# Interleaving VectorE's seven-product work across pairs, with more seven-product pairs: a two-layer decoder trunk on one core

## The chip, the cores and the metric

The kernel runs on one core of a Trainium2 chip. The metric is the device time in microseconds of one execution, given as the median of three runs. TensorE (PE) multiplies matrices, VectorE (DVE), ScalarE (ACT) and GpSimd (POOL) work elementwise, and SyncE (SP), like POOL, issues transfers. Every engine takes its instructions in the order of its own list and waits on semaphores for the others.

## The reference

The model has two layers on 256 positions of width 2048. Each layer is a token mixer (HGRN2 in the first, gated linear attention in the second) beside a cross-attention into 256 memory positions, an output projection, and a SwiGLU feed-forward of width 5632:

```python
h = x
for layer in range(DEPTH):
    hn = _rmsnorm(h, norm_mix[layer])
    ...
    h = h + jnp.concatenate([y, xa], axis=-1) @ w_out[layer]
    hn = _rmsnorm(h, norm_ffn[layer])
    gate, up = jnp.split(hn @ w_gate_up[layer], 2, axis=-1)
    h = h + (jax.nn.silu(gate) * up) @ w_down[layer]
return _rmsnorm(h, norm_final)
```

In the second mixer one input projection gives keys, queries, values, gates, a low-rank decay and the attention's queries. All is float32.

## The kernel before, in words

**Three matmuls for one product.** To keep float32 accuracy each operand is held as two fp32r tiles, a rounded high half and the rest as a low half. A product is three matmuls into one PSUM bank: high by high, high by low, low by high. The activations are split once. The weights stream in from HBM and every weight tile is split as it comes: ScalarE writes the high half (a cast), VectorE writes the low half (source minus high half). `split` (L276) does both. The result is a tile `parts`; the code names the splits of weight tile number i `parts{i}a` to `parts{i}d`.

**Seven products for eight.** A pair is 256 rows of weights by two column ranges of 512 (gate and up in the feed-forward; keys and queries, or two heads' columns, in a mixer), that is four 128x512 blocks in one tile `raw`. With the two halves of the 256 positions, a pair is a 2x2 by 2x2 product of blocks: eight products in the plain way. In the Strassen-Winograd way there are seven, each of 128 rows of weights, at the cost of sums of weight blocks. `seven` (L451) makes them: it splits the first block (part a) and the third and fourth (part b), subtracts the first block (`raw` 128x512), subtracts that from the third and fourth (`raw` 128x1024), and splits the results (part c with the sign turned, part d). For `fed` pairs the sum of two blocks is made on the way in, by a POOL transfer that adds to what an SP transfer has put there (L443, L444). For the first pair of a block, and for the last where it is of this kind, that sum sits in a tile of its own (`apart`, tile `T`), loaded long ahead.

A pair's kind is a letter. S is seven products, 21 matmuls. O is eight products from two splits. H is eight products too, but with sums that suit the banks of S; it takes splits a and b, one subtraction of 512 columns, and split c of that, 24 matmuls in all. In the mixers "-" is the plain form, 24 matmuls.

**Feed-forward.** `ffn` (L1208) goes over eleven blocks of 512 gate and 512 up columns. `up_block` calls `project_halves` (L624), which goes over the eight pairs of the block with the kinds in `KINDS` (L1197), one string each for the blocks 0, 1, 2 and 3 and one for all later blocks. The seven sums in PSUM are put together by `sums` (seven VectorE additions from PSUM), then gate times up is formed (`gate`), turned, and split as the left operand of the down projection. Two pieces of the down projection (`down`) follow each block from the second on; their weights are split into four or eight plain parts. In blocks 1 and 2 such a piece is 24 matmuls by two, later twice as long. The first block has no down projection behind it, and the second sums up the first block's products after its own first pair: `WHEN` says after which pair each of these works is due.

**What sets the order.** From the fourth pair of a layer's first block on, `Engine.kept` keeps each engine's instructions in the order in which the code is written. Elsewhere a scheduler may move them.

**Buffers.** `raw` has three buffers. Splits of two blocks share six buffers (`parts`); splits of one block, which are part a of an S pair and part c of an H pair, share two (tag `part`, L288). A cast into such a buffer waits until TensorE has used what was there before.

**Second mixer.** `gla_pair` (L1067) runs twice. Each run projects keys and queries for two heads with `project_two` (L549), 384 columns each, with the plan `------S-`: seven plain pairs and one S, in which the sum of two blocks is made by VectorE (`fed=False`).

Of the kernel before, what the change touches and what calls it, by code (L numbers as in the profile page):

```python
# [17 lines left out]
P = 128  # L18
# [22 lines left out]
def trunk_kernel(ctx: ExitStack, tc: tile.TileContext, x, mem, norm_mix, norm_ffn, norm_mem,  # L41
# [234 lines left out]
    def split(src, name, by=2, turned=False):  # L276

        if isinstance(src, list):
            both = wts.tile([P, 2, 2, 512], F32R, tag="parts", name=f"parts{name}", bufs=6)
            for k in (1, 0):  # L280
                hi = both[:, 0, k:k + 1, :]
                ac.activation(out=hi, in_=src[k], func=AF.Copy, scale=-1.0)
                ve.scalar_tensor_tensor(out=both[:, 1, k:k + 1, :], in0=src[k], scalar=-1.0, in1=hi.bitcast(F32),
                                        op0=ALU.mult, op1=ALU.subtract)
            return [(both[:, 0, k, :], both[:, 1, k, :]) for k in range(2)]
# [165 lines left out]
    def seven(i, raw, fed, between=None):  # L451

        n = raw.shape[2]
        tt = ve.tensor_tensor
        b00, = split(raw[:, 0:1, :], f"{i}a")
        b11, b10 = split(raw[:, 2:4, :], f"{i}b")
        if between:
            between()

        if not fed:  # L460
            tt(out=raw[:, 1, :], in0=raw[:, 1, :], in1=raw[:, 2, :], op=ALU.add)
        apart = fed if fed and fed is not True else None
        tt(out=raw[:, 0, :], in0=apart[:, 0, :] if apart else raw[:, 1, :], in1=raw[:, 0, :], op=ALU.subtract)
        tt(out=raw[:, 2:4, :], in0=raw[:, 2:4, :], in1=raw[:, 0:1, :].broadcast_to([P, 2, n]), op=ALU.subtract)
        t6, t7 = split([raw[:, 0:1, :], apart] if apart else raw[:, 0:2, :], f"{i}c", turned=True)
        t5, t4 = split(raw[:, 2:4, :], f"{i}d")
        return {1: ("x00", b00), 2: ("x01", b10), 3: ("z", b11), 4: ("x11", t4), 5: ("s", t5), 6: ("u", t6), 7: ("d0", t7)}
# [81 lines left out]
    def project_two(pairs, plan, w, c0, c1, n, name, give, view=lambda ps: ps, onto=None, prep=None, behind=None,  # L549
# [43 lines left out]
        for at, (p, kind) in enumerate(zip(order, plan)):  # L593
            i, raw = new_raw()
            if i == 0:
                load_pair(raw, w, p, c0, c1, n, kind, fed)
            if prep:
                prep(at)
            if i > 0:
                load_pair(raw, w, p, c0, c1, n, kind, fed)  # L600
            if kind == "S":
                todo = held(behind, seven, i, raw[:, :, 0:n], fed) if behind else seven(i, raw[:, :, 0:n], fed)
# [21 lines left out]
    def project_halves(forms, kinds, w, c0, c1, name, key, keep, apart):  # L624
# [15 lines left out]
        for p, kind in enumerate(kinds):  # L640
            Engine.kept = keep <= p
# [3 lines left out]
            fed = apart.get(p, True)  # L645
            load_pair(raw, w, p, c0, c1, 512, kind, fed)
            x = forms[p].get
            last = p == len(PAIRS) - 1
            if kind == "S":
                todo = seven(i, raw, fed, lambda: mark(key + p))  # L650
                for b in (1, 2, 6, 7, 5, 4, 3) if last else (1, 3, 2, 6, 7, 5, 4):
                    product(b, x(todo[b][0]), todo[b][1])
            else:
                b00, b01 = split(raw[:, 0:2, :], f"{i}a")
# [412 lines left out]
    def gla_pair(w, pr, dec, decay, hq, r, yq):  # L1067
# [46 lines left out]
        project_two(hq["pairs"], ("------S-", "------S-")[pr], w, kw + pr * 2 * DK, pr * 2 * DK, 2 * DK, f"gk{pr}", give,  # L1114
# [82 lines left out]
    KINDS = ("SHHSHOSO", "HHHSSOSO", "SHHSSOSO", "SSHSSOHS", "SSSSSOSS")  # L1197
# [10 lines left out]
    def ffn(l, forms, r, after, tail=None):  # L1208
# [9 lines left out]
        def up_block(b):  # L1218
# [5 lines left out]
            def sums():  # L1224
# [4 lines left out]
                for out, p, q in ((s0, 2, e0), (e1, 6, e0), (s1, 7, e1), (e1, 5, e1), (e0, 5, s1),  # L1229
                                  (s1, 4, s1), (e1, 3, e1)):  # L1230
                    ve.tensor_tensor(out=out, in0=ps[p], in1=q, op=ALU.add)
                    if p in (2, 5) and out is not e0 and b:
                        free_port.append(ve.last)
# [200 lines left out]
```

## Time and profile before

| what | before |
|---|---|
| median of three runs | 2255.65 us (2253.49 to 2257.12) |
| the profiled execution, its own time | 2254.6 us |
| its span, first to last instruction | 2252.8 us |
| granted TensorE clock | 0.999 |
| matmuls | 10668 |
| TensorE, VectorE, ScalarE, GpSimd busy | 99%, 90%, 64%, 12% of the span |
| feed-forward of the first layer | about 517 to 1181 us |
| feed-forward of the second layer | about 1560 to 2250 us |
| second mixer's two key/query stages | 1231.5 to 1275.6 and 1356.8 to 1392.3 us |

A row of the timeline has the start in microseconds, the length, the engine, the line, the operation, out<-in, the size, and in brackets how long the engine had been idle before it and who released it. Nearly all lines read L151, the helper through which every instruction is issued, so pieces are told apart by their tiles' names. `f_p` are the banks of the feed-forward's products and `hf_0` to `hf_7` the split activations of the eight pairs. Matmuls overlap, so the length of one row is longer than its share of time; the distance from start to start is what counts. Layer by layer the feed-forward has the same pattern, 204 weight tiles and 1043.3 us apart.

### The profile page before, as it was taken

Reading aid. Unit: us, or ns where it says so; the run is one execution under the profiler, and the core shown is the slowest. Engines: PE = TensorE matmul, PEld = TensorE weight load, DVE = VectorE, ACT = ScalarE, POOL = GpSimd, SP = SyncE. Lnnn points to the kernel's source line nnn. Section 1 sums busy time; section 2 is a strip of 40 time slices with the busy share of each in tenths; the row PEclk is TensorE's granted clock in tenths of the full one; section 3 lists DMA queues with packets and bytes.
Section 4 is the critical chain, followed back from the end, with each engine's and each line's share of the span. In section 5 each row is a group of like instructions: output and inputs, shape, how many; then the busy total and the mean of one; then the engine's idle time right before and its main releaser. Section 6 shows DMA issues by size and latency. Waiting matters only on the chain.

```text
span 2252.8 us, 30400 instructions
## 1 busy us (share of the span) xinstructions
PE 2238.6 (99%) x10668; PEld 1894.6 (84%) x10668; DVE 2031.5 (90%) x2551; ACT 1452.8 (64%) x2010; POOL 280.4 (12%) x275
## 2 busy tenths in 40 slices
PE   9999999999999999999999999999999999999998
PEld 7888888888888888888889999988888888888887
DVE  6879899898998999999996887889999999999997
ACT  7656656565666666666665665566566676666664
POOL 1000100000111112112210000000011221212110
PEclk9999999999999999999999999999999999999999
DMA  8656655656687778878865445566677878887874
GB/s 296 215 168 213 199 182 177 200 193 190 198 236 232 229 234 231 230 230 238 244 221 168 141 156 182 164 209 197 208 221 224 233 230 238 242 238 236 231 233 167
DMA packets 255628, 477.28 MB, mean 212 GB/s; under 512 B 18255, under 2 KB 47731, under 8 KB 255219
## 3 DMA queue, kind: packets, MB, share of 16 engines
q1 hardware_dynamic: 228547, 420.21, 55.5%
q0 software_dynamic: 25632, 50.87, 13.0%
q10 hardware_dynamic: 1296, 4.26, 0.5%
q8 instruction: 84, 1.38, 0.2%
q14 instruction: 69, 0.57, 0.1%
HBM read 472.12 MB, written 3.15 MB: 211 GB/s over the span
## 4 chain that ended last, share of the span: by engine, by line
PE 90%; DVE 6%; issue 2%; DMA 1%; ACT 1%; SPq 0%; POOL 0%; DVEq 0%; POOLq 0%; ACTq 0%
PE f_p L151 34%; PE fd L151 18%; PE wo L151 4%; PE m1p L151 2%; PE hv2p L151 2%; PE hv1p L151 2%; PE hf0p L151 2%; PE hv0p L151 2%; PE wo1p L151 2%; PE hf2p L151 2%; PE hf1p L151 2%; PE wo0p L151 2%; PE m0p L151 2%; PE gk0p L151 1%; PE gk1p L151 1%
## 5 line engine op out<-in xcount | busy, mean ns | idle before, releaser
L151 DVE TENSOR_TENSOR raw<-raw 128x1024 f32<-128x1024 f32 (+3 forms) x330 | 311.2, 943 | 16.7 <-DMA raw<-in_w_down_dram 5.6
L151 ACT CAST parts<-raw 128x1024 fp32r<-128x1024 f32 (+1 forms) x216 | 211.7, 1016 | 56.8 <-DMA raw<-in_w_down_dram 14.7
L151 DVE TENSOR_TENSOR parts<-raw,parts 128x1024 fp32r<-128x1024 f32 (+1 forms) x176 | 200.2, 1171 | 22.7 <-ACT parts L151 22.0
L444 POOL DMA_DIRECT2D raw<-in_w_gate_up_dram x92 | 80.4, 873 | 541.2 <-DMA raw<-in_w_gate_up_dram 274.7
L300 POOL TENSOR_TENSOR parts<-raw,parts 128x1024 fp32r<-128x1024 f32 x40 | 95.6, 2406 | 113.5 <-ACT parts L151 81.2
L151 ACT COPY h<-fd 128x512 f32<-128x512 f32 x80 | 45.7, 588 | 46.5 <-PE fd L151 44.0
L428 POOL DMA_DIRECT2D T<-in_w_gate_up_dram x36 | 21.1, 587 | 430.2 <-DVE hf_4g L151 82.7
L151 ACT ACTIVATE s<-s,rf_r 128x512 f32<-128x512 f32 x44 | 31.8, 723 | 42.0 <-DVE s L151 42.0
L151 DVE SCALAR_TENSOR_TENSOR s<-e,rf_r,s 128x512 f32<-128x512 f32 x44 | 45.7, 1076 | 2.9 <-ACT s L151 0.5
L151 DVE TENSOR_TENSOR e<-f_p,e 128x512 f32<-128x512 f32 x66 | 45.2, 684 | 2.6 <-DVE s L151 0.5
L429 POOL DMA_DIRECT2D T<-in_w_gate_up_dram x36 | 31.0, 861 | 120.4 <-DMA T<-in_w_gate_up_dram 111.1
L151 ACT COPY fd<-h 128x512 f32<-128x512 f32 x82 | 45.2, 582 | 0.0
L444 POOL DMA_DIRECT2D raw<-in_hgrn_w_in_dram x17 | 14.7, 867 | 209.9 <-DMA raw<-in_hgrn_w_in_dram 124.6
L151 PE MATMUL fd<-parts,s_0h 128*128 128x512 f32 x128 | 39.8, 392 | 0.0
L151 PE MATMUL fd<-parts,s_4h 128*128 128x512 f32 x128 | 39.8, 392 | 0.0
L151 PE MATMUL fd<-parts,s_8h 128*128 128x512 f32 x128 | 39.8, 392 | 0.0
L151 PE MATMUL fd<-parts,s_2h 128*128 128x512 f32 x128 | 39.8, 392 | 0.0
L151 PE MATMUL fd<-parts,s_6h 128*128 128x512 f32 x128 | 39.8, 392 | 0.0
L151 PE MATMUL fd<-parts,s_1h 128*128 128x512 f32 x128 | 39.4, 389 | 0.0
L151 PE MATMUL fd<-parts,s_3h 128*128 128x512 f32 x128 | 39.4, 389 | 0.0
L151 PE MATMUL fd<-parts,s_5h 128*128 128x512 f32 x128 | 39.4, 389 | 0.0
L151 PE MATMUL fd<-parts,s_7h 128*128 128x512 f32 x128 | 39.4, 389 | 0.0
(6020 smaller groups left out, 7434.0 us busy)
## 6 DMA issues: line engine op xcount, KB each, us to landing
raw<-in_w_gate_up_dram SPq DMA_DIRECT2D x224, 512.0 KB, 4.4
raw<-in_w_down_dram SPq DMA_DIRECT2D x80, 1024.0 KB, 5.5
raw<-in_w_gate_up_dram SPq DMA_DIRECT2D x220, 256.0 KB, 4.2
raw<-in_hgrn_w_in_dram SPq DMA_DIRECT2D x79, 512.0 KB, 4.6
raw<-in_gla_w_in_dram SPq DMA_DIRECT2D x96, 384.0 KB, 3.3
raw<-in_w_gate_up_dram POOLq DMA_DIRECT2D x92, 256.0 KB, 4.9
T<-in_w_gate_up_dram POOLq DMA_DIRECT2D x72, 256.0 KB, 5.0
raw<-in_w_out_dram SPq DMA_DIRECT2D x16, 1024.0 KB, 5.1
```

Of the source, the lines that this page charges most:

```text
L151: ins = func(*args, **kwargs)
L300: low = (nc.gpsimd if free_port else ve).tensor_tensor(out=both[:, 1, k:j, 0:m], in0=src[:, k:j, :], in1=both[:, 0, k:j, 0:m].bitcast(F32) ...
L428: nc.gpsimd.dma_start(out=both[:, 0, :], in_=rows[0])
L429: nc.gpsimd.dma_start(out=both[:, 0, :], in_=rows[1], accum_op=ALU.add)
L444: nc.gpsimd.dma_start(out=raw[:, 1, 0:n], in_=rows[1], accum_op=ALU.add)
```

## The change

It does five things.

1. In `seven`, the steps are put in another order, and the next pair is begun before this one is finished: after split c, a new argument `ahead` allocates and loads the next pair's tile and makes its split a; only then comes split d. A pair that was begun so goes on with the 512-wide subtraction before split b. The 1024-wide subtraction and split c change places with regard to what lies between them, so that no step stands right behind the one whose result it needs.
2. The same in H pairs: the next pair's split a stands between the subtraction and split c.
3. In `project_two`, an S pair that follows an S pair is begun early in the same way. This touches every stage that has two S pairs in a row.
4. `KINDS` gets two more S pairs in each of the blocks 0 and 1 and one more in each of the blocks 2 and 3 of both layers, each in the place of an H pair. The later blocks' string is the same. The two key/query stages get a second S pair in the place of a plain one.
5. `sums` takes bank 6 before bank 2 and swaps two later additions.

```diff
-    def seven(i, raw, fed, between=None):
+    def seven(i, raw, fed, between=None, b00=None, ahead=None):
...
-        b00, = split(raw[:, 0:1, :], f"{i}a")
...
+        def less():
+            tt(out=raw[:, 0, :], in0=apart[:, 0, :] if apart else raw[:, 1, :], in1=raw[:, 0, :], op=ALU.subtract)
+
+        def both_less():
+            tt(out=raw[:, 2:4, :], in0=raw[:, 2:4, :], in1=raw[:, 0:1, :].broadcast_to([P, 2, n]), op=ALU.subtract)
+
+        if not begun:
+            b00, = split(raw[:, 0:1, :], f"{i}a")
+        if not fed:
+            tt(out=raw[:, 1, :], in0=raw[:, 1, :], in1=raw[:, 2, :], op=ALU.add)
+        if fed and begun:
+            less()
         b11, b10 = split(raw[:, 2:4, :], f"{i}b")
         if between:
             between()
...
+        if not (fed and begun):
+            less()
+        if apart:
+            t6, t7 = split([raw[:, 0:1, :], apart], f"{i}c", turned=True, between=both_less)
+        else:
+            both_less()
+            t6, t7 = split(raw[:, 0:2, :], f"{i}c", turned=True)
+        if ahead:
+            ahead()
         t5, t4 = split(raw[:, 2:4, :], f"{i}d")
...
+        def ahead(p):
+            if p < len(PAIRS):
+                i, raw = come(p)
+                came.append((i, raw, split(raw[:, 0:1 if kinds[p] == "S" else 2, :], f"{i}a")))
...
                     ve.tensor_tensor(out=raw[:, 3, :], in0=raw[:, 3, :], in1=raw[:, 2, :], op=ALU.subtract)
+                    ahead(p + 1)
                     e1, = split(raw[:, 3:4, :], f"{i}c")
...
-        project_two(hq["pairs"], ("------S-", "------S-")[pr], w, kw + pr * 2 * DK, pr * 2 * DK, 2 * DK, f"gk{pr}", give,
+        project_two(hq["pairs"], "-----SS-", w, kw + pr * 2 * DK, pr * 2 * DK, 2 * DK, f"gk{pr}", give,
...
-    KINDS = ("SHHSHOSO", "HHHSSOSO", "SHHSSOSO", "SSHSSOHS", "SSSSSOSS")
+    KINDS = ("SHSSSOSO", "SHSSSOSO", "SSHSSOSO", "SSSSSOHS", "SSSSSOSS")
...
-                for out, p, q in ((s0, 2, e0), (e1, 6, e0), (s1, 7, e1), (e1, 5, e1), (e0, 5, s1),
+                for out, p, q in ((e1, 6, e0), (s0, 2, e0), (s1, 7, e1), (e0, 5, s1), (e1, 5, e1),
```

What this does to the order is shown at three places of the first layer. Weight tiles 84 to 91 are the pairs of its block 0, 92 to 99 those of block 1, 102 to 109 those of block 2.

VectorE in block 0, from the fourth pair (87) on; `hf0_7g` and `hf0_7l` are steps of the last pair's activations. Before:

```order
L151 TENSOR_TENSOR parts87a_4541<-raw87_4536,parts87a_4541 128x512
L151 TENSOR_TENSOR hf0_7g_4488<-hf0_7g_4488 128x256
L151 SCALAR_TENSOR_TENSOR hf0_7g_4488<-hf0_7g_4488 128x128
L151 TENSOR_TENSOR hf0_7g_4488<-hf0_7g_4488 128x128
L151 TENSOR_TENSOR parts87b_4544<-raw87_4536,parts87b_4544 128x1024
L151 TENSOR_TENSOR hf0_7l_4482<-hf0_7g_4488,hf0_7h_4481 128x1024
L151 TENSOR_TENSOR raw87_4536<-raw87_4536 128x512
L151 TENSOR_TENSOR hf0_7g_4488<-hf0_7g_4488 128x128
L151 TENSOR_TENSOR raw87_4536<-raw87_4536 128x1024
L151 SCALAR_TENSOR_TENSOR parts87c_4549<-raw87_4536,parts87c_4549 128x1024
L151 TENSOR_TENSOR hf0_7l_4482<-hf0_7g_4488,hf0_7h_4481 128x128
L151 TENSOR_TENSOR parts87d_4552<-raw87_4536,parts87d_4552 128x1024
```

And after:

```order
L151 TENSOR_TENSOR parts87a_4520<-raw87_4515,parts87a_4520 128x512
L151 TENSOR_TENSOR raw87_4515<-raw87_4515 128x512
L151 TENSOR_TENSOR hf0_7g_4496<-hf0_7g_4496 128x256
L151 TENSOR_TENSOR parts87b_4548<-raw87_4515,parts87b_4548 128x1024
L151 SCALAR_TENSOR_TENSOR hf0_7g_4496<-hf0_7g_4496 128x128
L151 TENSOR_TENSOR raw87_4515<-raw87_4515 128x1024
L151 TENSOR_TENSOR hf0_7g_4496<-hf0_7g_4496 128x128
L151 SCALAR_TENSOR_TENSOR parts87c_4552<-raw87_4515,parts87c_4552 128x1024
L151 TENSOR_TENSOR parts88a_4560<-raw88_4555,parts88a_4560 128x512
L151 TENSOR_TENSOR parts87d_4563<-raw87_4515,parts87d_4563 128x1024
L151 TENSOR_TENSOR hf0_7l_4490<-hf0_7g_4496,hf0_7h_4489 128x1024
L151 TENSOR_TENSOR raw88_4555<-raw88_4555 128x512
```

The first split of pair 88, now an S pair, stands ahead of the last split of pair 87, and the longest step of the activations has moved behind it.

VectorE in block 1, from split a of its fourth pair (95) on, which was and is an S pair; `s0_0l` belongs to block 0's down projection. Before:

```order
L151 TENSOR_TENSOR parts95a_4861<-raw95_4856,parts95a_4861 128x512
L151 TENSOR_TENSOR parts95b_4864<-raw95_4856,parts95b_4864 128x1024
L151 TENSOR_TENSOR s0_0l_4819<-tp_s0_0h_48180_4820,s0_0h_4818 128x512
L151 TENSOR_TENSOR raw95_4856<-raw95_4856 128x512
L151 TENSOR_TENSOR raw95_4856<-raw95_4856 128x1024
L151 SCALAR_TENSOR_TENSOR parts95c_4871<-raw95_4856,parts95c_4871 128x1024
L151 TENSOR_TENSOR parts95d_4874<-raw95_4856,parts95d_4874 128x1024
L151 TENSOR_TENSOR parts96a_4905<-raw96_4900,parts96a_4905 128x512
```

And after:

```order
L151 TENSOR_TENSOR parts95a_4854<-raw95_4849,parts95a_4854 128x512
L151 TENSOR_TENSOR parts94d_4857<-raw94_4799,parts94d_4857 128x1024
L151 TENSOR_TENSOR raw95_4849<-raw95_4849 128x512
L151 TENSOR_TENSOR parts95b_4882<-raw95_4849,parts95b_4882 128x1024
L151 TENSOR_TENSOR s0_0l_4839<-tp_s0_0h_48380_4840,s0_0h_4838 128x512
L151 TENSOR_TENSOR raw95_4849<-raw95_4849 128x1024
L151 SCALAR_TENSOR_TENSOR parts95c_4888<-raw95_4849,parts95c_4888 128x1024
L151 TENSOR_TENSOR parts96a_4896<-raw96_4891,parts96a_4896 128x512
L151 TENSOR_TENSOR parts95d_4899<-raw95_4849,parts95d_4899 128x1024
L151 TENSOR_TENSOR raw96_4891<-raw96_4891 128x512
```

The two `raw` steps are apart, and between split c and split d of a pair stands split a of the next.

ScalarE in block 2, around the pairs 105 and 106. Before:

```order
L151 CAST parts105a_5288<-raw105_5283 128x512
L151 CAST parts105b_5291<-raw105_5283 128x1024
L151 ACTIVATE parts105c_5296<-raw105_5283 128x1024
L151 CAST parts105d_5299<-raw105_5283 128x1024
L151 CAST parts106a_5328<-raw106_5323 128x512
```

And after:

```order
L151 CAST parts105a_5279<-raw105_5274 128x512
L151 CAST parts104c_5282<-raw104_5240 128x512
L151 CAST parts105b_5310<-raw105_5274 128x1024
L151 ACTIVATE parts105c_5314<-raw105_5274 128x1024
L151 CAST parts106a_5322<-raw106_5317 128x512
L151 CAST parts105d_5325<-raw105_5274 128x1024
```

The cast of parts106a, whose buffer is one of the two, has moved ahead of that of parts105d. The second layer has the same orders, with the tiles' numbers 204 higher.

More of the change, by code (lines that the diff above doesn't have):

```diff
@@ L591, in early, with come @@
                 out[:] = onto
[L593 removed]
+        came = []
+        def come(at):
             i, raw = new_raw()
             if i == 0:
[L596 removed]
+                load_pair(raw, w, order[at], c0, c1, n, plan[at], fed)
             if prep:
@@ L649, in project_halves @@
             if kind == "S":
-                todo = seven(i, raw, fed, lambda: mark(key + p))
+                todo = seven(i, raw, apart.get(p, True), lambda: mark(key + p), begun and begun[0], lambda: ahead(p + 1))
                 for b in (1, 2, 6, 7, 5, 4, 3) if last else (1, 3, 2, 6, 7, 5, 4):
@@ L653, in project_halves @@
             else:
-                b00, b01 = split(raw[:, 0:2, :], f"{i}a")
+                b00, b01 = begun or split(raw[:, 0:2, :], f"{i}a")
                 mark(key + p)
```

37 lines of the change are left out of this document (23 added, 14 removed).

## The prediction

> All times are microseconds of the one core; a pair is named by the number of its weight tile (raw 84 is the first of the first feed-forward layer), its parts by the letters of the code.
>
> **What bounds the kernel now.** First the page: which engine is busy, and for how long.
>
> ```profile
> span 2252.8 us, 30400 instructions
> ...
> PE 2238.6 (99%) x10668; PEld 1894.6 (84%) x10668; DVE 2031.5 (90%) x2551; ACT 1452.8 (64%) x2010; POOL 280.4 (12%) x275
> ```
>
> TensorE is taken all the time and VectorE nearly so. Whether TensorE waits inside its 99% is told by the chain of waits: length by number of matmuls.
>
> ```profile
> 729.83 38.81 PE f_p L151 x171
> ...
> 1367.88 24.47 PE gk1p L151 x141
> ```
>
> 38.81 / 171 = 0.227 for a 512-wide matmul, 24.47 / 141 = 0.173 for a 384-wide one, with nothing between them. There each matmul left out is time won, as long as VectorE delivers the parts in time. So the second view is VectorE's timeline, for one seven-product pair (S) where such pairs follow one another:
>
> ```profile
> 733.78 0.68 DVE L151 TENSOR_TENSOR parts126a<-raw,parts126a 128x512 fp32r<-128x512 f32 x1
> 734.38 1.22 DVE L151 TENSOR_TENSOR parts126b<-raw,parts126b 128x1024 fp32r<-128x1024 f32 x1
> 735.51 1.94 DVE L151 TENSOR_TENSOR raw<-raw 128x512 f32<-128x512 f32 x2
> 737.46 1.23 DVE L151 SCALAR_TENSOR_TENSOR parts126c<-raw,parts126c 128x1024 fp32r<-128x1024 f32 x1
> 738.65 1.23 DVE L151 TENSOR_TENSOR parts126d<-raw,parts126d 128x1024 fp32r<-128x1024 f32 x1
> 739.79 0.68 DVE L151 TENSOR_TENSOR parts127a<-raw,parts127a 128x512 fp32r<-128x512 f32 x1
> ```
>
> From start to start a 512-wide step takes 0.60 and a 1024-wide one 1.14. The pair lasts 6.01, of which 2 x 0.60 + 4 x 1.14 = 5.76 is the steps; 0.25 goes where a step needs the one just before it (the two raw steps take 1.95, not 1.74). TensorE needs 21 x 0.227 = 4.77 for the same pair: in a run of S pairs VectorE loses 1.2 a pair, and lives on the lead it gains in the down projections. The third view is the same for an eight-product pair (H):
>
> ```profile
> 568.11 1.23 DVE L151 TENSOR_TENSOR parts94a<-raw,parts94a 128x1024 fp32r<-128x1024 f32 x1 [0.26 <-ACT parts94a L151]
> 569.25 1.22 DVE L151 TENSOR_TENSOR parts94b<-raw,parts94b 128x1024 fp32r<-128x1024 f32 x1
> 570.50 0.69 DVE L151 TENSOR_TENSOR raw<-raw 128x512 f32<-128x512 f32 x1
> 571.96 0.69 DVE L151 TENSOR_TENSOR parts94c<-raw,parts94c 128x512 fp32r<-128x512 f32 x1 [0.77 <-ACT parts94c L151]
> 572.57 0.69 DVE L151 TENSOR_TENSOR parts95a<-raw,parts95a 128x512 fp32r<-128x512 f32 x1
> ```
>
> 4.46, with 2 x 1.14 + 2 x 0.60 = 3.48 of steps; the rest is waiting for ScalarE. TensorE needs 24 x 0.227 = 5.45 for it. And the place where VectorE's lead is spent, a few pairs on, on TensorE's timeline:
>
> ```profile
> 584.26 0.50 PE L151 MATMUL f_p<-parts96c,hf_4h 128*128 128x512 f32 x1 [0.35 <-DVE parts96c L151]
> ...
> 586.90 0.61 PE L151 MATMUL f_p<-parts97a,hf_5h 128*128 128x512 f32 x2
> ```
>
> TensorE waits for parts96c: in the second block VectorE is the one that comes last, and it is only just in time. (The wait falls on a part's second matmul, which takes the low half that VectorE writes.) So two engines bound this kernel: TensorE nearly everywhere, VectorE in the first two blocks of each layer, where the change puts eight of its twelve new S pairs.
>
> **What it removes.** An H pair made S drops a product, three matmuls: 12 pairs x 3 x 0.227 = 8.2. The two key/query stages drop one product each: 2 x 3 x 0.173 = 1.04. Together 9.2, all on the path if the parts are in time.
>
> **What it adds, first two blocks.** By the steps above an S pair costs VectorE 5.76 (interleaved) where the H pair cost 4.46, and an H pair that stays falls to 3.48. What that makes is counted over the stretch from parts87a, the first part of the fourth pair, to the end of pair 96.
>
> ```profile
> 528.30:586.50 58.20, 57.85 (x258) 47.19 (x258) 53.47 (x62) 34.63 (x43) 3.47 (x4) 1.00 0.59 182
> ```
>
> ```profile
> 528.31 0.69 DVE L151 TENSOR_TENSOR parts87a<-raw,parts87a 128x512 fp32r<-128x512 f32 x1 [1.32 <-ACT parts87a L151]
> ...
> 558.28 0.68 DVE L151 TENSOR_TENSOR s<-f_p,e 128x512 f32<-128x512 f32 x1
> ...
> 564.53 1.22 DVE L151 TENSOR_TENSOR parts93b<-raw,parts93b 128x1024 fp32r<-128x1024 f32 x1
> ...
> 585.32 1.22 DVE L151 TENSOR_TENSOR parts97a<-raw,parts97a 128x1024 fp32r<-128x1024 f32 x1
> ```
>
> Before, VectorE took 58.2 from 528.31 to the end of parts97a (586.54), for 30 steps of 1024, 26 of 512 and five short ones of the last forms (1.2 together, an estimate by width from the 0.60): 34.2 + 15.6 + 1.2 = 51.0. The other 7.2 were waits (the row above has VectorE busy for 53.47 of 58.20; a record reaches some 0.09 into the next one). In the new order parts97a stands ahead of parts96d, so the stretch ends with parts96d; it holds 35 of 1024, 28 of 512 and the same five: 39.9 + 16.8 + 1.2 = 57.9. So the waits that interleaving wins back are eaten by the added steps. I leave 0.9 of waits in it: 0.2 in pair 90, which follows an O pair and is not begun early; about 0.15 in H pair 93; and 0.5 in the sums and gate, which take 6.25 before (558.28 to 564.53) for nine steps of 0.60, and lose a little by their new order. That makes 58.8. From below the waits can be 0, from above the 7.2 of before; I take 0.9 since the waits in the rows above are all of the kinds that the new order parts.
>
> The start shifts too. Parts a of an S pair and part c of an H pair share two buffers (tag "part"). Before, parts87a took the buffer of parts85c:
>
> ```profile
> 527.65 0.62 ACT L151 CAST parts87a<-raw 128x512 fp32r<-128x512 f32 x1 [1.93 <-PE f_p L151]
> ...
> 624.76 0.62 ACT L151 CAST parts105a<-raw 128x512 fp32r<-128x512 f32 x1 [1.04 <-PE f_p L151]
> ```
>
> Now it takes that of parts86a, which is free three matmuls (0.68) into pair 86:
>
> ```profile
> L151 PE MATMUL f_p<-parts86a,hf_2h x8: 387/394/476, 527.8 to 530.2; 128*128 128x512 f32 x8
> ```
>
> So its cast starts at 528.5 instead of 527.65, with the copies of the last form and parts87c queued behind it on ScalarE, and VectorE starts at about 529.2. 529.2 + 58.8 = 588.0: parts96d is complete. TensorE can start its first matmul 0.23 before that and needs six (1.36) to finish the pair: 589.2 against 586.90 before, **2.3 later**. Without VectorE it would have been 4 x 0.68 = 2.7 earlier; 5.0 of waits take the place. What is late next is parts c and d, put back by the 0.60 or 1.14 of the next pair's first split.
>
> **Third block.** One more S pair: 0.68 less. VectorE has lead here, but after H pair 104 the two buffers bind: parts106a must wait for TensorE's first product from parts105a, and parts105d now stands behind it on ScalarE and VectorE.
>
> ```profile
> 629.96 0.62 PE L151 MATMUL f_p<-parts105a,hf_3h 128*128 128x512 f32 x2
> ```
>
> With 2.3 of delay and 0.68 saved pair 105 starts at 631.5 and frees the buffer at 632.2. ScalarE casts 106a (0.62, as in the row above) and 105d (about 1.1, an estimate from twice the width), to 633.9; VectorE then does 105d, raw 0.60, 106b, raw, 106c, 107a, 106d: 6 x 1.14 + 0.60 more, 641.3. TensorE would want parts106d's low half at 631.5 + 4.77 + 5 x 0.68 + 0.23 = 639.9. A wait of 1.35, so +0.67 in all; between 0 (the lead suffices) and 2.
>
> **Fourth block**: 0.68 less, no H pair ahead of two S pairs, VectorE's lead large: -0.68. **Later blocks** have the same pairs as before: each S pair is 0.25 shorter, part d comes 0.6 to 1.1 later; nothing to win, since TensorE does not wait there. Sum for a layer: 2.3 + 0.67 - 0.68 = +2.3, for both +4.6.
>
> **Key/query stages.** The first one's busy row (PE, PEld, DVE, ACT, POOL after the length), and its steps:
>
> ```profile
> 1231.00:1276.00 45.00, 45.00 (x260) 43.64 (x259) 34.45 (x60) 29.10 (x50) 1.09 (x3) 1.00 0.44 140
> ```
>
> ```profile
> 1273.73 0.55 DVE L151 TENSOR_TENSOR gsk<-gk0p,gsq 128x384 f32<-128x384 f32 x1
> 1274.19 0.95 DVE L151 TENSOR_TENSOR parts232b<-raw,parts232b 128x768 fp32r<-128x768 f32 x1
> ```
>
> The new S pair needs three 384-wide (0.46) and four 768-wide (about 0.87) steps, 4.9, for the two 768-wide ones before, 1.7: +3.1 on an engine with 10.5 idle in 45. I take them as hidden: -1.04 for both; at worst two thirds uncovered, +2; at best, with the final adds no longer mixed with the decay chain, -2.
>
> **Transfers and queues.** A feed-forward pair made S has one more issue on SP and an accumulating one on POOL:
>
> ```profile
> raw<-in_w_gate_up_dram SPq DMA_DIRECT2D x220, 256.0 KB, 4.2
> ...
> raw<-in_w_gate_up_dram POOLq DMA_DIRECT2D x92, 256.0 KB, 4.9
> ```
>
> 4.2 + 4.9 and the hand-over is some 10 from the release of the tile; between release and use lie two pairs, 3.48 + 5.76 = 9.2 at the shortest, and in the first and second block the sums or the early load besides. Nothing, at most 0.8 a place without that cover. The other S runs (first mixer, output, memory) are interleaved too; TensorE does not wait there, so nothing.
>
> **The sum.** The profiled execution took 2254.6, 1.8 beyond its span. +4.6 - 1.04 = +3.5: 2258.1. The median of the runs is 2255.65, 1.05 above the profiled one; on its scale **2259.2**. That is +0.16%; a measurement of this kernel tells about 0.2% (4.5) from nothing. Case chance 0.56, own range 2254 to 2264.
>
> **Rivals.** (1) Faster: VectorE keeps up and the 9.2 arrive, 2246.5. For it: the blocks from the fifth on carry seven S pairs each with TensorE unbroken (38.81 for 171), and 7.2 of waits lie in the stretch. Against it: the count, 57.9 of pure steps where TensorE would be done at 584.2. It needs parts96d 5 earlier. 0.18, part of it only halfway (2251).
> (2) Slower, by the two buffers: in each chain H, S, S of the first three blocks the second S is held as in the third. One wait of 1.35 is counted; two more a layer are 2 x 2.7 = 5.4: 2264.6. It decides if the cast of parts95a starts after TensorE's first product from parts94a rather than right after parts94c's cast. For it: both bracketed rows <-PE f_p. Against it: by the count VectorE reaches parts95a about 1 after that product. 0.14.
> (3) Slower: taking needy neighbours apart wins nothing, S stays 6.01 and H 4.46. Five begun S pairs (0.25) and one H (1.0) in the stretch, one S after it, 2.5 a layer: 2264.2. Against it: the raw steps' 1.95 for 1.74. 0.12.
> The Trainium skill ("VectorE: DVE Perf Modes", The DRAIN you can't avoid) speaks for this: the next VectorE operation waits for the pipe to empty whatever it needs, and a semaphore between two costs nothing more. The rows do not agree: the step behind one that it needs starts 0.2 later.
>
> **How the numbers follow.** The forecast's case lies within 2251.1 to 2260.2 for 0.36 of its 0.56; rival 1 gives 0.17 below and the rest inside; rivals 2 and 3 and the forecast's remainder lie above. Faster 0.17, same 0.38, slower 0.45. The range leaves out the lower half of rival 1 and the worst of leftover waits (3 more a layer): 2249 to 2267.
>
> **What would show it.** TensorE waiting for parts87d to 88d and 94c to 96d in both layers, some 5 a layer; parts96d complete near 588 if the span's start is alike; parts106a's cast held by TensorE; f_p unbroken in the fourth block and later. Wrong if parts96d comes before 584, if the waits stand at parts a or b (transfers), or if the key/query stages move by more than 2.

## The result, and the profile after

The changed kernel takes **2272.3 us** (median of five runs, 2270.75 to 2273.87), the kernel before 2255.65: ratio 1.0078, 95% interval 1.0064 to 1.0092. The forecast was 2259.2, its range ended at 2267. Slower was its likeliest side, but the size was wrong, and the largest part of the loss lies where the prediction had put nothing.

The page of the changed kernel (span; then busy time, share and instructions of each engine) says little by itself:

```profile
span 2272.0 us, 30459 instructions
...
PE 2241.0 (99%) x10626; PEld 1883.1 (83%) x10626; DVE 2053.3 (90%) x2587; ACT 1465.7 (65%) x2028; POOL 295.2 (13%) x289
```

42 matmuls are gone, as planned, and TensorE is at 99% as before; the span is 19.2 longer. Where that comes from is told by the windows, cut at the first matmul of the same weight tiles: 84 to 102 (the first two blocks), 102 to 112 (the third), 112 to 124 (the fourth), 124 to 208 (the seven later ones). Columns: start:end, length, busy time and instructions of PE, PEld, DVE, ACT, POOL, granted clock, DMA share, GB/s. The first layer before:

```profile
516.80:614.30 97.50, 97.15 (x439) 79.86 (x438) 87.57 (x105) 61.23 (x81) 9.56 (x8) 1.00 0.62 196
614.30:666.90 52.60, 52.60 (x238) 43.63 (x237) 47.83 (x52) 35.25 (x47) 10.35 (x9) 1.00 0.79 236
666.90:729.70 62.80, 62.80 (x283) 52.09 (x282) 56.66 (x63) 40.19 (x52) 11.63 (x12) 1.00 0.79 236
729.70:1159.90 430.20, 430.20 (x1926) 356.56 (x1925) 408.56 (x441) 290.60 (x369) 80.48 (x73) 1.00 0.80 234
```

And after:

```profile
517.80:618.20 100.40, 96.67 (x427) 77.07 (x426) 95.49 (x114) 64.30 (x86) 16.35 (x14) 1.00 0.71 211
618.20:672.50 54.30, 52.91 (x235) 42.87 (x235) 49.35 (x53) 36.22 (x47) 10.45 (x9) 1.00 0.75 224
672.50:736.40 63.90, 62.90 (x279) 51.25 (x278) 58.71 (x65) 41.05 (x53) 11.93 (x11) 1.00 0.78 231
736.40:1169.80 433.40, 432.15 (x1927) 356.12 (x1926) 406.08 (x441) 292.19 (x371) 80.87 (x73) 1.00 0.79 234
```

The first layer is longer by 2.9, 1.7, 1.1 and 3.2, the second, cut at the same tiles, by 3.0, 1.1, 1.1 and 2.8: 16.9 in all, about the 16.65 between the medians. The last row is the one to read twice. In the later blocks the strings are the same, VectorE is busy for 2.5 *less* than before, and the stretch is 3.2 longer. No work was added there; it is done in another order.

The chain of waits (start, length, what) of the changed kernel shows the place. Where it ran through 171 matmuls at a stretch before, it now crosses to VectorE once in each later block:

```profile
758.14 1.23 DVE parts128d L151
759.42 16.43 PE f_p L151 x71
...
821.33 16.43 PE f_p L151 x71
```

Parts128d is the last part of the last of five S pairs in a row; an O pair (129) follows. VectorE's timeline before, and TensorE's first use of that part:

```profile
750.70 1.23 DVE L151 TENSOR_TENSOR parts128d<-raw,parts128d 128x1024 fp32r<-128x1024 f32 x1
751.84 1.22 DVE L151 TENSOR_TENSOR parts129a<-raw,parts129a 128x1024 fp32r<-128x1024 f32 x1
```

```profile
752.14 0.62 PE L151 MATMUL f_p<-parts128d,hf_4h 128*128 128x512 f32 x2
```

The part was complete at 751.93, 0.2 ahead of its first matmul and, with 0.23 from matmul to matmul, 0.4 ahead of the second, which takes the low half. So before there was no wait, but hardly a lead either. The same places after:

```profile
757.01 1.22 DVE L151 TENSOR_TENSOR parts129a<-raw,parts129a 128x1024 fp32r<-128x1024 f32 x1
758.14 1.22 DVE L151 TENSOR_TENSOR parts128d<-raw,parts128d 128x1024 fp32r<-128x1024 f32 x1
```

```profile
758.87 0.39 PE L151 MATMUL f_p<-parts128d,hf_4h 128*128 128x512 f32 x1
759.42 0.50 PE L151 MATMUL f_p<-parts128d,hf_4h 128*128 128x512 f32 x1 [0.16 <-DVE parts128d L151]
```

The next pair's split a takes the turn of split d, which starts 1.13 after it. The matmul that needs the low half comes 0.33 late and the one behind it 0.11 more: 0.44 in a block, seven blocks, two layers, 6.2. The changed kernel pays this for a part (129a) that is first used 2.5 after it is complete.

### The profile page after: what moved, and what is told of

Read it like the earlier page. It is cut to its first block, busy times and chain, and to the rows that moved or that the text cites. A ratio compares the mean times of both kernels' runs of the same rounds, so it can differ in the third digit from the quotient of the medians.

```text
span 2272.0 us, 30459 instructions
## 1 busy us (share of the span) xinstructions
PE 2241.0 (99%) x10626; PEld 1883.1 (83%) x10626; DVE 2053.3 (90%) x2587; ACT 1465.7 (65%) x2028; POOL 295.2 (13%) x289
## 4 chain that ended last, share of the span: by engine, by line
PE 48%; DVE 16%; issue 8%; DMA 3%; ACT 2%; SPq 0%; ACTq 0%; DVEq 0%; POOLq 0%; POOL 0%
PE fd L151 17%; PE f_p L151 16%; DVE raw L151 3%; PE wo L151 2%; PE wo1p L151 2%; DMA raw<-in_w_gate_up_dram 2%; PE gg11p L151 1%; PE gg01p L151 1%; PE gg10p L151 1%; PE gk1p L151 1%; PE gx L151 1%; PE gk0p L151 1%; PE fd_0p L151 1%; DMA raw<-in_w_down_dram 1%; DVE parts L151 0%
## 5 line engine op out<-in xcount | busy, mean ns | idle before, releaser
L151 DVE TENSOR_TENSOR raw<-raw 128x512 f32<-128x512 f32 (+2 forms) x346 | 328.1, 949 | 21.1 <-DMA raw<-in_w_down_dram 7.8
L446 POOL DMA_DIRECT2D raw<-in_w_gate_up_dram x102 | 88.3, 865 | 609.7 <-DVE raw L151 303.1
L430 POOL DMA_DIRECT2D T<-in_w_gate_up_dram x38 | 24.5, 645 | 339.4 <-DVE ro_v L151 56.9
L151 DVE SCALAR_TENSOR_TENSOR s<-e,rf_r,s 128x512 f32<-128x512 f32 x44 | 54.1, 1269 | 2.5
L431 POOL DMA_DIRECT2D T<-in_w_gate_up_dram x38 | 32.8, 862 | 128.5 <-DMA T<-in_w_gate_up_dram 99.7
```

The lines of the kernel that those rows point to most:

```text
L151: ins = func(*args, **kwargs)
L430: nc.gpsimd.dma_start(out=both[:, 0, :], in_=rows[0])
L431: nc.gpsimd.dma_start(out=both[:, 0, :], in_=rows[1], accum_op=ALU.add)
L446: nc.gpsimd.dma_start(out=raw[:, 1, 0:n], in_=rows[1], accum_op=ALU.add)
```

## The experiments

The table has the lengths of the eight stretches, cut as above, from each run's own trace, one execution each; "before" in a run's text is the median of the kernel before on the same chip.

| kernel | first layer | second layer | sum |
|---|---|---|---|
| before | 97.5, 52.6, 62.8, 430.2 | 97.3, 52.8, 62.8, 430.5 | 1286.5 |
| the change | 100.4, 54.3, 63.9, 433.4 | 100.3, 53.9, 63.9, 433.3 | 1303.4 |
| the new order alone | 98.6, 55.4, 64.0, 433.2 | 99.5, 54.0, 64.0, 433.1 | 1301.8 |
| the added pairs alone | 101.2, 51.9, 62.8, 430.5 | 101.1, 52.0, 64.6, 430.3 | 1294.4 |
| S pairs begin only S pairs early | 99.7, 53.1, 63.0, 430.6 | 99.7, 52.9, 63.1, 430.1 | 1292.2 |
| the same with the old strings | 96.8, 52.9, 63.1, 430.1 | 96.7, 53.0, 63.1, 430.5 | 1286.2 |
| 1024-wide step between the halves of split c | 97.4, 52.5, 62.9, 432.0 | 97.3, 52.5, 62.9, 432.2 | 1289.7 |
| H pairs only, tile 103 made S | 96.8, 51.9, 62.8, 432.4 | 96.7, 52.2, 62.8, 432.3 | 1287.9 |
| the same, old order inside S | 96.7, 51.9, 62.8, 430.1 | 96.8, 51.9, 62.7, 430.5 | 1283.4 |
| the same, tile 88 made S too | 96.0, 52.7, 62.7, 430.6 | 96.1, 51.9, 62.7, 430.2 | 1282.9 |
| the change, H pairs only | 98.2, 51.9, 64.3, 432.3 | 98.5, 51.9, 64.3, 432.2 | 1293.6 |
| the change, split c of H pairs in a wide buffer | 99.7, 54.9, 63.9, 433.2 | 99.2, 54.1, 63.9, 433.2 | 1302.1 |
| key/query pairs alone | 97.3, 52.6, 62.7, 430.4 | 97.3, 53.9, 62.8, 430.4 | 1287.4 |
| key/query pairs, third and fourth block | 97.3, 52.2, 62.8, 430.2 | 97.3, 51.9, 63.1, 430.2 | 1285.0 |

**The new order alone.**

```diff
-    KINDS = ("SHSSSOSO", "SHSSSOSO", "SSHSSOSO", "SSSSSOHS", "SSSSSOSS")
+    KINDS = ("SHHSHOSO", "HHHSSOSO", "SHHSSOSO", "SSHSSOHS", "SSSSSOSS")
```

and the key/query plan of before.

> The changed kernel with the kinds of pairs of before (feed-forward strings and key/query plan); only the order is new. Theory A (two costs: a next pair's split a ahead of split d makes d late at the end of every run of S pairs; and added S pairs overfill VectorE): the seven later blocks of each layer lose 0.44 each as in the changed kernel, 6.2 in all, at TensorE's wait for part d of their fifth pair, and the chains H, S, S of the second to fourth block lose up to 1.9 each by the held split a: 2262 to 2270. Theory B (only the added S pairs cost; the order is neutral or better): 2252 to 2256, with no wait at part d in the later blocks.

2271.18 (before 2255.84): ratio 1.0059, interval 1.0045 to 1.0072: against theory B, and a little above theory A's range. The order by itself costs nearly all that the change costs. The wait at the fifth pair of each later block is there:

```profile
759.54 0.50 PE L151 MATMUL f_p<-parts128d,hf_4h 128*128 128x512 f32 x1 [0.17 <-DVE parts128d L151]
```

**The added pairs alone**, in the order of before (the change's strings and plan in the kernel before).

> The kernel before with the new strings and the new key/query plan, each pair in the old order. Theory A: no wait in the later blocks; an S pair costs VectorE 1.55 more than the H pair it replaces (6.01 for 4.46), three of them in the stretch to the end of pair 96 whose lead is used up: 4 to 5 later per layer there, the third block about 0, the fourth up to 0.7 later, key/query 1.0 earlier: 2262 to 2267. Theory B: the old order loses more than the new, so above the changed kernel's 2272. Theory C (the order alone is at fault): the products left out arrive, 2247 to 2251.

2261.26 (before 2255.84): 1.0024, 1.0015 to 1.0033; a little under theory A's range, far from B and C. The later blocks are untouched. The loss is in the first two blocks (+3.7 and +3.8); in the third each layer wins 0.7 to 0.8; the fourth wins nothing in the first layer and loses 1.8 in the second. The list of TensorE's waits (who, for whom: us, times, longest):

```profile
PE f_p L151 <- DVE parts95c L151: 0.8, 1, 0.8
PE f_p L151 <- DVE parts299c L151: 0.8, 1, 0.8
...
PE f_p L151 <- DVE parts94c L151: 0.8, 1, 0.8
...
PE f_p L151 <- DVE parts88c L151: 0.8, 1, 0.8
```

These are waits for part c in the blocks where VectorE had no lead. The two effects overlap: 15.3 and 5.4 apart, 16.6 together.

**S pairs begin only S pairs.**

```diff
-  ... begun and begun[0], lambda: ahead(p + 1))
+  ... begun and begun[0], (lambda: ahead(p + 1)) if kinds[p + 1:p + 2] == "S" else None)
```

> The changed kernel, but an S pair begins the next pair ahead of its own split d only where the next is an S pair too; ahead of an O or H pair split d comes first, as before. Theory A: the 0.44 of each later block goes (6.2 in all), and of the waits for the last part d of a run in the first four blocks (88d, 96d, 106d, 116d: 0.78, 0.79, 0.78, 0.76) up to 3.1 a layer: 2260 to 2266. Theory B: VectorE's count of steps is the same, so 2270 to 2273.

2262.75 (before 2255.84): 1.0029, 1.0019 to 1.0039, within theory A's range. Of the 16.65 above the kernel before 6.9 are left: 9.7 (11.2 of the 16.9 in the table) are gone by this one condition, with VectorE busy for 2053.1, as with the change (2053.3). The 6.9 are near the 5.4 of the added pairs alone. At the end of the run the two splits stand the old way round, and the later blocks take 430.6 and 430.1:

```profile
754.06 1.22 DVE L151 TENSOR_TENSOR parts128d<-raw,parts128d 128x1024 fp32r<-128x1024 f32 x1
755.21 1.22 DVE L151 TENSOR_TENSOR parts129a<-raw,parts129a 128x1024 fp32r<-128x1024 f32 x1
```

**The same condition with the strings and the plan of before.**

> The strings and the key/query plan of before, and the new order with an S pair begun early only by an S or H pair, an O or H pair never begun ahead of split d of an S pair. By the waits of the run with the new order alone: 0.44 at each of fourteen later blocks goes, and 0.52, 0.78, 0.76 and 0.76 at parts 87d, 96d, 106d and 116d of each layer, 11.8 in all: 2259 to 2262, with the waits at 105c, 105d and 106c left. If the order loses by something else (transfers asked for later, the sums' new order): 2265 to 2271.

2257.88 (before 2254.9): 1.001, 1.0001 to 1.0018; better than expected by 1. It is 3.0 above its own before where the new order alone was 15.3 above its own, so 12.4 of what the order costs by the medians, and all that it costs in the table's stretches, hang on beginning an O or H pair ahead of split d. The new order of the sums (item 5) and the early S pairs of the mixers (item 3) were not run alone; this kernel has both, and with all that is left of the order it is 3.0 slower. No wait over 0.24 is left in the first layer's `f_p`; a new one stands in the first layer's last down projection (0.7 in the second layer's):

```profile
PE fd_0p L151 <- DVE parts210c L151: 1.3, 1, 1.3
```

**The second S pair of the key/query stages alone.**

> The kernel before with the second S pair in the two key/query stages alone. Theory A (VectorE's idle time there covers it): 1.0 less, 2254.6, the stage 43.6 long for 44.1. Rival (the added 3.1 of VectorE's work delays what follows, the value stage above all): 2255.5 to 2257.

2256.95 (before 2255.84): 0.9999, 0.9991 to 1.0008: no gain that can be told. The stages show what happens. The first and the stretch behind it, before:

```profile
1231.50:1275.50 44.00, 44.00 (x254) 42.86 (x254) 33.45 (x58) 28.60 (x49) 1.09 (x3) 1.00 0.43 137
...
1275.50:1356.80 81.30, 79.71 (x482) 77.47 (x481) 72.73 (x129) 53.81 (x83) 1.73 (x4) 1.00 0.52 168
```

and in the changed kernel:

```profile
1240.60:1284.10 43.50, 43.50 (x251) 42.20 (x250) 33.87 (x59) 28.58 (x50) 1.09 (x3) 1.00 0.44 141
1284.10:1366.70 82.60, 80.93 (x481) 77.27 (x481) 74.47 (x132) 54.70 (x85) 1.74 (x4) 1.00 0.51 165
```

In the changed kernel 0.5 is won in the stage and 1.3 lost behind it; with this edit alone the two are 44.0 and 82.0. The loss behind it does not come each time: cut at the stage's own matmuls, the run with the added pairs alone, which has the same edit, takes 43.4 and 81.5 where the kernel before takes 43.8 and 81.5. Its cause is not shown.

**Split c of an H pair in a wide buffer.**

```diff
-                    e1, = split(raw[:, 3:4, :], f"{i}c")
+                    e1, = split(raw[:, 3:4, :], f"{i}c", wide=True)
```

> The changed kernel, but split c of an H pair takes one of the six wide buffers, so that the two small ones serve the parts a of S pairs alone. If the hold by the two buffers is what the third block loses by, the cast of parts106a starts right behind parts105c, and of the waits at parts b, c and d of pair 106 (0.21, 0.88 and 0.78) some 1.2 goes in each layer: 2269 to 2271. If VectorE's count and split d behind the next split a are the cause there too: 2271.5 to 2273.

2271.1 (before 2254.9): 1.0065, 1.0049 to 1.0081, not to be told from the change. The hold is gone, and something else takes its place. In the change the third block has, on ScalarE and VectorE,

```profile
633.45 0.62 ACT L151 CAST parts106a<-raw 128x512 fp32r<-128x512 f32 x1 [2.56 <-PE f_p L151]
```

```profile
637.20 0.69 DVE L151 TENSOR_TENSOR raw<-raw 128x512 f32<-128x512 f32 x1 [0.92 <-DMA raw<-in_w_gate_up_dram]
```

and here

```profile
631.17 0.62 ACT L151 CAST parts106a<-raw 128x512 fp32r<-128x512 f32 x1 [1.80 <-DMA raw<-in_w_gate_up_dram]
```

```profile
636.38 0.69 DVE L151 TENSOR_TENSOR raw<-raw 128x512 f32<-128x512 f32 x1 [2.37 <-DMA raw<-in_w_gate_up_dram]
```

The cast no longer waits for TensorE, and VectorE waits 2.37 instead of 0.92 for the tile's accumulating transfer. Tile 106 takes the memory of tile 103, which is free when split d of 103 is done, and that split, too, stands behind the next split a in this order. Counted from the first matmul of tile 84 this subtraction of tile 106 starts after 119.4 in both kernels, so the buffers were one of two equal limits there. That the place of split d makes the transfer late was not tested. The transfer can come late without the change too: in the run with the key/query pairs alone, which leaves this block as it was, VectorE waited for it in the second layer,

```profile
1679.22 1.95 DVE L151 TENSOR_TENSOR raw<-raw 128x512 f32<-128x512 f32 x2 [1.46 <-DMA raw<-in_w_gate_up_dram]
```

and that layer's third block took 53.9 for 52.8. Differences of 1 in this block are therefore not put down to an edit without such a row.

**Only H pairs begin the next pair early**, with the strings of the change.

> The new strings and plan; only H pairs begin the next pair early, S pairs do not, and split c of an H pair has a wide buffer. If beginning a pair early inside a run of S pairs is worth its 0.14 a pair, this is no better than the run with S pairs begun only ahead of S pairs (2262.75); if the delay of split d by 0.6 costs more than that, it is at or below the run with the added pairs alone: 2258 to 2261.

2265.27 (before 2254.9): 1.0042, 1.0028 to 1.0056. This is no better than 2262.75, as the first theory said, and worse than the added pairs alone. But its later blocks took 432.3 and 432.2, where nothing begins early and nothing was added: something else in the order inside S pairs costs time too. The next run shows the same with only one pair added in each layer.

**H pairs only, old strings, and one S pair more (tile 103).** The sums and the key/query plan are those of before, and split c of an H pair has a wide buffer.

> The kernel before with H pairs alone beginning the next pair early, split c of an H pair in a wide buffer, and one added S pair: the second of the third block (tile 103), where no wait followed it in the run with the added pairs alone. 0.68 a layer for the product and 0.6 a layer for the wait at 96c: 2253 to 2254.5. If the lead at 103 is spent elsewhere: 2255 to 2258.

2260.52 (before 2254.9): 1.0025, 1.0016 to 1.0034, where a gain was expected. The table divides it: the first three blocks win 1.4 and 1.2 as expected, the later ones lose 2.2 and 1.8. In each later block's last pair, whose sum lies in its own tile `T`, VectorE has

```profile
764.36 1.22 DVE L151 TENSOR_TENSOR raw<-raw 128x1024 f32<-128x1024 f32 x1
765.50 0.69 DVE L151 SCALAR_TENSOR_TENSOR parts131c<-raw,parts131c 128x512 fp32r<-128x512 f32 x1
766.78 1.23 DVE L151 TENSOR_TENSOR parts131d<-raw,parts131d 128x1024 fp32r<-128x1024 f32 x1 [0.60 <-ACT parts131d L151]
```

The 1024-wide subtraction now stands between the two halves of split c. ScalarE can cast for split d only after it, and one 512-wide step (0.60) does not cover a cast of 1.05. Before, two such steps did.

**That edit alone**, in the kernel before.

```diff
-        tt(out=raw[:, 2:4, :], in0=raw[:, 2:4, :], ...)
-        t6, t7 = split([raw[:, 0:1, :], apart] if apart else raw[:, 0:2, :], f"{i}c", turned=True)
+        if apart:
+            t6, t7 = split([raw[:, 0:1, :], apart], f"{i}c", turned=True, between=both_less)
+        else:
+            both_less()
+            t6, t7 = split(raw[:, 0:2, :], f"{i}c", turned=True)
```

> The kernel before with one edit: in an S pair whose sum has a tile of its own, the 1024-wide subtraction stands between the two halves of split c instead of ahead of both. If that exposes ScalarE's cast for split d (VectorE waited 0.60 for it at parts131d in the run with H pairs alone begun early), d comes 0.5 later, where TensorE had 0.19 to spare: some 0.3 in each of the later blocks and less in the fourth, so 4 to 5 in all, 2259 to 2261. If the lost time there came with something else: 2255 to 2257.

2261.71 (before 2255.67): 1.003, 1.0019 to 1.0042. The wait is there, 0.59 at split d for ScalarE, with ScalarE's cast at 766.01, behind a subtraction that VectorE began at 764.68 and ended at 765.90. The later blocks lose 1.8 and 1.7, over half of the 6.0. Of the rest, 0.9 is a wait for parts210c in the first layer's last down projection; what remains was not traced to a cause. In the changed kernel the next pair's split a covers this wait at a block's first pair, but not at its last (0.60 at parts131d there too). Whether VectorE's wait reaches TensorE depends on the lead: with S pairs begun early only ahead of S pairs, and the old strings, it is there as well (0.59), and the later blocks take 430.1 and 430.5, as before.

**H pairs only, tile 103, and the order of before inside S pairs.**

> The run with H pairs alone begun early and one more S pair (tile 103), but inside an S pair all steps in the order of before (both subtractions behind split b, the 1024-wide one ahead of both halves of split c). If the 0.3 in each later block and the wait at parts 210c (1.9) came from those two edits, they go: 1.5 won in the first three blocks of each layer stays, 2252 to 2254.5. If beginning a pair early in H pairs is itself at fault: above 2257.

2251.88 (before 2255.67): 0.9988, 0.9979 to 0.9997. This version beats both kernels. Two parts of the change pay in it, which the table tells apart: the first two blocks, where H pairs begin the next pair early and no pair was added, are 0.8 and 0.5 shorter, and the third, with tile 103, 0.7 and 0.9, as with the added pairs alone. `f_p` has no wait left in the first three blocks:

```profile
568.32 0.68 DVE L151 TENSOR_TENSOR parts95a<-raw,parts95a 128x512 fp32r<-128x512 f32 x1
569.17 0.69 DVE L151 TENSOR_TENSOR parts94c<-raw,parts94c 128x512 fp32r<-128x512 f32 x1 [0.17 <-ACT parts94c L151]
```

In an H pair the next split a fills the 0.77 in which VectorE waited for ScalarE's cast of split c; split c comes 0.60 later in the order and was not needed at once. There the early step fills a wait; ahead of split d at the end of a run of S pairs it displaces a part that is needed at once.

**The pairs of the third and fourth block and of the key/query stages, in the old order.**

> The kernel before, in its old order, with the added S pairs of the third and fourth block and of the two key/query stages, and none in the first two blocks. If the added pairs cost only where VectorE has no lead (3.6 and 3.8 in the first two blocks of the layers, by the run with all added pairs): 0.6 a layer won in the third block, nothing in the fourth, 0.5 in each key/query stage: 2253 to 2255. If the key/query pairs give back what they win, as in the run of their own: 2254 to 2256.

2254.8 (before 2255.67): 0.9998, 0.9989 to 1.0007; no difference that can be told. The third blocks win 0.4 and 0.9, the fourth nothing, and in this run what the key/query stages win is lost behind them.

**One S pair more on top of the best version (tile 88).**

> The run with H pairs alone begun early, the old order inside S pairs and the S pair at tile 103, and one more: pair 88 of the first block. By that run's trace VectorE is over 3.2 ahead of TensorE all through the first block and 2.17 at parts96c; the pair takes 2.2 more of VectorE and 0.68 less of TensorE. If the lead is made new between the blocks (VectorE waits there for buffers), no wait comes up at 96c and 0.68 a layer is won: 2250.5. If the loss is carried through the second block, parts96c comes 0.7 late and nothing is won: 2252.

2251.81 (before 2255.13): 0.9986, 0.9976 to 0.9995, no different from the run without it. The first two blocks are 0.7 shorter in both layers (96.0 and 96.1), with no wait at 96c; in the first layer the third block is 0.8 longer, behind a wait of 0.97 for tile 106's transfer:

```profile
634.48 1.95 DVE L151 TENSOR_TENSOR raw<-raw 128x512 f32<-128x512 f32 x2 [0.97 <-DMA raw<-in_w_gate_up_dram]
```

TensorE then waits 0.45 for parts106c. Since that wait for the transfer comes and goes without this edit, and the second layer's third block took 51.9 as without it, whether the pair pays is left open.

## Why the prediction was wrong, step by step

| part, both layers | forecast | measured |
|---|---|---|
| first two blocks | +4.6 | +5.9 |
| third block | +1.3 | +2.8 |
| fourth block | -1.4 | +2.2 |
| later blocks | 0 | +6.0 |
| key/query stages | -1.0 | -1.0 |
| between the stretches | 0 | +0.6 |
| start and end of the profiled run | 0 | +2.7 |
| span | +3.5 | +19.2 |

The medians differ by 16.65, 2.5 less than the spans of the two profiled executions. The 1.0 at the start varies with the run (the first matmul of tile 84 stands at 517.9 with the key/query pairs alone, an edit that lies behind it, and at 516.8 before); what the 1.7 at the end is was not traced.

**The step that failed** is "Later blocks ... part d comes 0.6 to 1.1 later; nothing to win, since TensorE does not wait there". It had the delay right and made no sum of it. The views that it read, a chain with 171 unbroken matmuls and S pairs of 6.01 against 4.77, say that TensorE came last; they do not say by how much. Two rows more would have: 1.2 lost in each of five pairs uses up a lead, and at parts128d only 0.4 of it was left at the matmul that takes the low half. Counted from the block's first matmul (729.7 and 736.4), split d starts at 21.0 before and at 21.7 after: of the 1.13 the shorter pairs ahead of it won back 0.4, and the 0.7 that remained is more than the lead. The count that was made with care for the first two blocks, where VectorE was seen to be late, was not made where it was on time.

**The fourth block** failed in the same way ("VectorE's lead large"). Before, the last S pair ahead of its O pair (116) had these rows:

```profile
687.91 1.23 DVE L151 TENSOR_TENSOR parts116d<-raw,parts116d 128x1024 fp32r<-128x1024 f32 x1
```

```profile
690.01 0.62 PE L151 MATMUL f_p<-parts116d,hf_4h 128*128 128x512 f32 x2
```

A lead of 0.9 at the first matmul and 1.1 at the one that takes the low half; the added S pair takes 1.4 or more from VectorE and 0.68 from TensorE's need, and split d stands 1.1 later, behind a 1024-wide split. After:

```profile
694.60 0.50 PE L151 MATMUL f_p<-parts116c,hf_4h 128*128 128x512 f32 x1 [0.40 <-DVE parts116c L151]
...
696.87 0.50 PE L151 MATMUL f_p<-parts116d,hf_4h 128*128 128x512 f32 x1 [0.60 <-DVE parts116d L151]
```

**The first two blocks** went by the mechanism that was told, VectorE overfull, with the waits at 88b to 88d and 94c to 96d, and came out 0.6 or 0.7 a layer dearer. Two errors partly cancel. The rows, of ScalarE first:

```profile
528.70 0.62 ACT L151 CAST parts87a<-raw 128x512 fp32r<-128x512 f32 x1 [1.14 <-PE f_p L151]
...
529.35 0.69 DVE L151 TENSOR_TENSOR parts87a<-raw,parts87a 128x512 fp32r<-128x512 f32 x1 [0.54 <-ACT parts87a L151]
...
588.27 1.22 DVE L151 TENSOR_TENSOR parts96d<-raw,parts96d 128x1024 fp32r<-128x1024 f32 x1
```

With the start of this run 1.0 later, parts87a begins on VectorE as before (528.35), not at 529.2. TensorE does hold its cast, but by parts85c, whose last matmul ends at 528.7, as it did before, and not by parts86a as the prediction had it: the buffer comes free where it did. And the stretch takes 60.1, not 58.8: 2.2 of waits are left in it and not 0.9. Parts96d is complete at 588.5 on the old scale, against the 588.0 forecast.

**The third block** has the hold by two buffers and the place that were told, at more than the price: 2.4 of waits in the first layer and 1.8 in the second (what the block lost, and the 0.68 saved), and not 1.35. Behind the hold stood the transfer of tile 106, 0.92 late, for which the prediction had put "nothing"; without the hold it decides alone. How much of it belongs to the change is open, since it was seen without the change as well.

**The key/query stages** won 0.5 each, as forecast; the stretch behind the first was 1.3 longer, which not every run with the edit shows.

**The rivals.** (1) is out: VectorE did not keep up. (2) the hold by the buffers was one cost of the third block, and gave way to a transfer when it was taken away; it did not spread to the second block, where the cast of parts95a, by which the prediction wanted to decide, starts right behind that of parts94c. (3) is half out: an S pair in a run takes 5.87, not 6.01 and not 5.76, and H pairs gained by being taken apart. What neither the forecast nor a rival had is a loss by order alone, in blocks to which nothing was added: 15.3 with the old strings, 12.4 of it undone by one condition.

The rule of the Trainium skill that stood beside rival 3 ("VectorE: DVE Perf Modes", The DRAIN you can't avoid) does not agree with these rows either: in the last section neighbours that do not need each other start 1.14 apart, 0.08 before the record of the first ends, and a third kind 0.11 later. The section of the skill adds that a next operation that is not held starts earlier, which the 1.14 does not contradict.

## What to carry to other kernels

A chain of waits that stays on one engine tells who is last, not how far ahead the others are; before a step is put ahead of another, read when the displaced one is ready and when it is used, at the end of each run, where the lead is smallest. A step moved forward pays where it fills a wait (here ScalarE's cast, in H pairs); ahead of the last part of a run it takes a busy engine's time from the part that is needed next, and a loss of 0.44 that repeats in fourteen blocks outweighs the two blocks that are studied closely. Where one limit is taken away, look for the second limit right behind it.

## What the hardware showed

The gaps between VectorE's steps depend on how two neighbours are related. In the changed kernel's run of S pairs:

```profile
745.27 0.68 DVE L151 TENSOR_TENSOR parts127a<-raw,parts127a 128x512 fp32r<-128x512 f32 x1
...
747.61 1.22 DVE L151 TENSOR_TENSOR parts127b<-raw,parts127b 128x1024 fp32r<-128x1024 f32 x1
748.86 1.22 DVE L151 TENSOR_TENSOR raw<-raw 128x1024 f32<-128x1024 f32 x1
750.00 1.22 DVE L151 SCALAR_TENSOR_TENSOR parts127c<-raw,parts127c 128x1024 fp32r<-128x1024 f32 x1
751.14 0.68 DVE L151 TENSOR_TENSOR parts128a<-raw,parts128a 128x512 fp32r<-128x512 f32 x1
```

The step behind a 1024-wide one follows it after 1.14 (748.86 to 750.00, 750.00 to 751.14), but the subtraction that overwrites what split b has just read comes 1.25 after it. Where another step stands between the two, as in

```profile
577.26 1.21 DVE L151 TENSOR_TENSOR parts95b<-raw,parts95b 128x1024 fp32r<-128x1024 f32 x1
578.40 0.68 DVE L151 TENSOR_TENSOR s_0l<-tp_s_0h,s_0h 128x512 fp32r<-128x512 f32 x1
579.00 1.21 DVE L151 TENSOR_TENSOR raw<-raw 128x1024 f32<-128x1024 f32 x1
```

the steps follow after 1.14 and 0.60. So in these rows overwriting what a neighbour read costs 0.11; reading what it wrote cost 0.2 in the kernel before (the two raw steps of pair 126, 1.95 for 1.74). The new order trades the one for the other: an S pair takes 5.87 (745.27 to 751.14) for 6.01, and wins 0.14 where the prediction counted 0.25.
